# Raw weights cast on GpSimd, and the factors of the mixing fetched on GpSimd's queue

## The chip, the core and the metric

The kernel runs on one core of a Trainium2 chip. The core has five engines with a queue of instructions each: TensorE (PE, matrix products and transposes; its weight loads are shown as PEld), VectorE (DVE), ScalarE (ACT), GpSimd (POOL), and SyncE (SP), which here only issues DMAs. Each queue is worked off in its order; an instruction that waits for a semaphore holds up what stands behind it on the same queue. The metric is the device time of one execution in microseconds, smaller is better.

## The reference

One layer of a hybrid decoder for a prompt of 2048 tokens and 8 sample tokens, model width 1024, float32 in and out:

```python
h = einsum('bsd,de->bse', x, w_in)          # q, k, v and gate of two mixers
# mixer A: 8 heads, banded attention (128) at dilations 1, 4 and 16,
#   the three partial results merged by their softmax denominators
# mixer B: 8 query / 2 key heads, window 128, a learned sink per head
mix = concat([oa * silu(ga), ob * silu(gb)])
y = layer_norm(ALPHA * x + mix @ w_o) * ln_g + ln_b
```

The keys and values are outputs as well. The sample tokens attend to a cache; the 2048 prompt tokens hold nearly all of the work.

## The kernel before, in words

Products of float32 quality are made of three products of a faster format: each operand is split into a high part `h` (a cast to that format) and a low part `l` (the operand less its high part), and `h*h + h*l + l*h` is summed in PSUM. Every weight tile therefore needs a cast and a subtraction before PE can use it.

The kernel has four stages. Up to 244 us it projects the first ten column tiles of the input projection, to about 386 us the values and the sample tokens of mixer A, to about 1062 us runs the attention stage, and then the output projection with the normalisation.

The attention stage is written out by hand (`manual_schedule`): every engine's queue holds its instructions in the order of the program text. Its main loop (lines 1121 to 1151) runs over blocks: for each head pair and each dilation four blocks, 12 blocks for a pair of mixer A (four pairs) and 4 for a pair of mixer B (four pairs). In a block PE makes the scores (L823), DVE masks them and finds the extremes (L831), ACT takes the exponentials (L834), PE transposes them (L853), DVE or ACT copies the transposes from PSUM (L859, L857), and PE multiplies by the values (L874). Each block has four steps; in each step PE is also given a share of other work (`advance`), which is the projection of the remaining tiles (`stream`, products at L629), and then `step()` is called. This first calls `tick`, which calls `raw_step` and issues stores that are due, and then moves each running chain (a Python generator) one `yield` further.

Three of these are touched by the change or by the prediction:

- **Raw weights.** `stream` makes three passes over the tokens, with four, four and three weight tiles; `out_weights` and `late_wo` later need the eight tiles of the output projection. 17 of these tiles come through the class `Parts` in four pieces of 128x256. `raw_step` (L129) keeps up to four pieces (`RAW`) in flight: it has SP load a piece into the buffer `raw` (L142), and three ticks later, when the tile's place is free, DVE casts it into `h` (L137) and POOL subtracts (L138). When PE needs a tile that is not complete yet, the text forces the rest. The first two tiles of a set have places named `gw`, the next ones `gw2` and `gw3`; the tiles of a new set take the places of the old one while its last chunk of tokens is projected.
- **Mixing of a pair of mixer A** (`merge_a`, L1001). From the statistics DVE and ACT compute a factor for each token and dilation; SP stores the factors to DRAM (`fd`, L1028). They are fetched back in eight chunks of 256 tokens, each spread over 64 partitions for each of the two heads: two DMAs of 64 x 3 x 256 numbers a chunk (L1038) into the buffer `F`, of which there are two. POOL multiplies the three partial results by the factors and adds them: five instructions a chunk (L1050, L1052, L1053). After two ticks the fetch of the chunk after next follows, and SP stores the mixed chunk (`ms`, L1058) one tick later.
- **Mixing of a pair of mixer B** (`merge_b`, L944). It has one factor a token, three chunks of 768, 768 and 512 tokens and two DMAs a chunk (L980). POOL multiplies (L990), DVE the second chunk, and all of the last pair.

SP issues all DMAs of the kernel in one queue: besides those named, the tokens of the projection (`gx`, L581), keys, queries and values (L898, L906, L772 to L782), the gates (L175) and the statistics (L935, L940).

Of the kernel before, what the change touches and what calls it, by code (L numbers as in the profile page):

```python
# [18 lines left out]
SEQ = 2048  # L19
# [27 lines left out]
def dram(t, off, ap):  # L47
    return bass.AP(tensor=t.tensor, offset=t.offset + off, ap=[list(a) for a in ap])
# [3 lines left out]
def hymba_step(ctx, tc, xt, xs, xr, wq, wv, wo, tab, msk, ident, diag, sinks, lng, lnb,  # L52
               kca, vca, kcb, vcb, y, kto, vo):
    nc = tc.nc
    V, S, G, T = nc.vector, nc.scalar, nc.gpsimd, nc.tensor
    dma = nc.sync.dma_start
# [36 lines left out]
    def tick(last=False):  # L93
        slot[0] += 1
        raw_step()
        while due and (last or any(d.at <= slot[0] for d in due)):
            now = [d for d in due if last or d.at <= slot[0]]
            due[:] = [d for d in due if d not in now]
            for d in now:
                d.run()  # L100

    def soon(fn, steps=2):
        return Later(fn, steps) if steady else fn()
# [10 lines left out]
    class Parts:  # L114
# [9 lines left out]
        def __iter__(self):  # L124
            while self.left:
                raw_step(True)
            return iter(self.hl)

    def raw_step(now=False):  # L129

        for r in raws:
            r[4] += r[3] is not None
        for _ in range(2):
            if raws and raws[0][0].hl and raws[0][3] is not None and (now or raws[0][4] >= 3):
                p, _, k0, w, _ = raws.popleft()
                h, l = p.hl
                V.tensor_copy(h[:, k0:k0 + 2], w)  # L137
                G.tensor_sub(l[:, k0:k0 + 2], w, h[:, k0:k0 + 2].bitcast(F32))  # L138
                p.left -= 1
        for r in [r for r in islice(raws, RAW) if r[3] is None][:2]:  # L140
            r[3] = at.tile([128, 2, 128], F32, name="raw", bufs=RAW)
            dma(r[3], r[1][:, r[2]:r[2] + 2])  # L142
# [83 lines left out]
    with tc.tile_pool(name="wp", bufs=2) as wp, tc.tile_pool(name="pw", bufs=2) as pw:  # L226
# [13 lines left out]
        def x_of(ci, kt):  # L240
            return [t[:, kt % 2] for t in X5[kt // 2]] if ci == 6 else [t[:, kt] for t in X[ci]]
# [80 lines left out]
        for oi, i in enumerate(order):  # L322
            for ci in range(7):
                if oi == 0 and ci < 6:
                    load_x(ci + 1)
                n = 7 * oi + ci
# [5 lines left out]
                c0, n = CHUNKS[ci]  # L332
# [157 lines left out]
    with xscope, tc.tile_pool(name="spa", bufs=1, reuse_waits="tile") as sp, \  # L490
# [9 lines left out]
        for gi, (h0, w) in enumerate(VG):  # L500
            wvh, wvl = wvp[gi]
            for tb in VO[gi]:
# [19 lines left out]
                for kt in () if new else range(8):  # L522
                    ci = max(i for i in range(7) if CHUNKS[i][0] <= tb * 128)
                    t0 = tb * 128 - CHUNKS[ci][0]
                    a, b = [t[:, t0:t0 + 128] for t in x_of(ci, kt)]
# [418 lines left out]
    def merge_b(job):  # L944

        m, den = job.of.st[:, 0, :, 0], job.of.st[:, 0, :, 1]
        sk = snk[:, 2 * job.of.pair:2 * job.of.pair + 2, None].to_broadcast([128, 2, 16])
        mn = at.tile([128, 2, 16], F32, name="mn", bufs=1)
        w = at.tile([128, 2, 2, 16], F32, name="wts", bufs=1)
        dn = at.tile([128, 2, 16], F32, name="dn", bufs=1)  # L950
        V.scalar_tensor_tensor(mn, sk, -1.0, m, op0=OP.mult, op1=OP.min)
        V.tensor_sub(w[:, 0], mn, m)
        V.tensor_add(w[:, 1], mn, sk)
        S.activation(w, w, AF.Exp)
        yield
        V.tensor_mul(dn, w[:, 0], den)
        V.tensor_add(dn, dn, w[:, 1])
        V.reciprocal(dn, dn)
        V.scalar_tensor_tensor(w[:, 0], w[:, 0], 0.5, dn, op0=OP.mult, op1=OP.mult)
        while where[0] < 3:  # L960
            yield
        pst = ps.tile([128, 512], F32, name="pst", tag="pt", bufs=1)
        T.transpose(pst[:32, :128], w[:, 0].rearrange("p a b -> p (a b)"), idt)
        stT = at.tile([64, 128], F32, name="stT")
        V.tensor_copy(stT[:32], pst[:32, :128])
        yield
        for h in range(2):
            dma(job.of.fd[h, 0].rearrange("(r b i) -> b r i", r=16, b=16),
                stT[16 * h:16 * h + 16].rearrange("n (r i) -> n r i", r=16))
        yield  # L970
        yield
        fd = job.of.fd
        kt, o = 4 + job.of.pair, job.of.o[1]
        Fs = []

        def fetch(c):
            F = at.tile([128, 768], F32, name="F", bufs=2)
            n = min(768, SEQ - 768 * c)
            for a in range(2):
                dma(F[a * 64:a * 64 + 64, :n], dram(fd, a * SEQ + c * 768, [[0, 64], [1, n]]))  # L980
            Fs.append(F[:, :n])

        fetch(0)
        fetch(1)
        yield
        yield
        yield
        for c in range(3):
            cc = slice(c * 768, min(c * 768 + 768, SEQ))
            (V if c == 1 or kt == 7 else G).tensor_mul(o[:, cc], o[:, cc], Fs[c])  # L990
            yield
            if c == 0:
                fetch(2)
            if c == 1:
                yield
            if kt < 6:
                soon(lambda kt=kt, cc=cc, o=o: dma(ms[kt, :, cc], o[:, cc]), 1)
        merged.append(kt)
        resident.append(o)

    def merge_a(job):  # L1001

        fd, oT = job.of.fd, job.of.o
        sc = at.tile([128, 2, 3, 2, 16], F32, name="sc", bufs=1)
        yield
        yield
        dma(sc.rearrange("p a b c e -> p (a b c) e"), job.of.sd.rearrange("a b c (p e) -> p (a b c) e", e=16))
        yield
        yield
        yield  # L1010
        mn = at.tile([128, 2, 16], F32, name="mn", bufs=1)
        dn = at.tile([128, 2, 16], F32, name="dn", bufs=1)
        w = at.tile([128, 2, 3, 16], F32, name="wts", bufs=1)
        V.tensor_tensor(mn, sc[:, :, 0, 0], sc[:, :, 1, 0], op=OP.min)
        V.tensor_tensor(mn, mn, sc[:, :, 2, 0], op=OP.min)
        for pi in range(3):
            V.tensor_sub(w[:, :, pi], mn, sc[:, :, pi, 0])
        S.activation(w, w, AF.Exp)
        yield
        V.tensor_mul(dn, w[:, :, 0], sc[:, :, 0, 1])  # L1020
        for pi in range(1, 3):
            V.tensor_mul(mn, w[:, :, pi], sc[:, :, pi, 1])
            V.tensor_add(dn, dn, mn)
        V.reciprocal(dn, dn)
        for pi in range(3):
            V.scalar_tensor_tensor(w[:, :, pi], w[:, :, pi], 0.5, dn, op0=OP.mult, op1=OP.mult)
        yield
        dma(fd.rearrange("a c (p e) -> p (a c) e", e=16), w.rearrange("p a c e -> p (a c) e"))  # L1028
        yield
        yield  # L1030
        yield
        kt = job.of.pair
        Fs = []

        def fetch(c):
            F = at.tile([128, 3, 256], F32, name="F", bufs=2)
            for a in range(2):
                dma(F[a * 64:a * 64 + 64],  # L1038
                    dram(fd, a * 3 * SEQ + c * 256, [[0, 64], [SEQ, 3], [1, 256]]))
            Fs.append(F)  # L1040

        fetch(0)
        fetch(1)
        yield
        yield
        for c in range(8):
            cc = slice(c * 256, c * 256 + 256)
            F = Fs[c]
            m = oT[PA[0]][:, cc]
            G.tensor_mul(m, m, F[:, 0])  # L1050
            for pi, d in enumerate(PA[1:]):
                G.tensor_mul(F[:, 1 + pi], oT[d][:, cc], F[:, 1 + pi])  # L1052
                G.tensor_add(m, m, F[:, 1 + pi])  # L1053
            yield
            yield
            if c < 6:
                fetch(c + 2)
            soon(lambda kt=kt, cc=cc, m=m: dma(ms[kt, :, cc], m), 1)  # L1058
        ready.append(kt)
# [103 lines left out]
    with tc.tile_pool(name="ol", bufs=1, reuse_waits="tile") as ol:  # L1163
# [7 lines left out]
        for i, tb in enumerate([16] + list(range(16))):  # L1171
# [3 lines left out]
            if tb in first:  # L1175
                x, n = first[tb]
# [159 lines left out]
```

## Time and profile before

| | |
|---|---|
| median of the runs | 1244.24 us (3 runs, 1241.34 to 1249.01) |
| profiled execution | 1243.91 us, span of its instructions 1242.1 us |
| mean granted clock of TensorE | 0.978 |
| POOL's busy time, attention stage (386 to 1062 us) | 176.97 of 676 us |
| PE's busy time, attention stage | 606.41 of 676 us |
| DMA | one queue, 228.66 MB, 184 GB/s from and to HBM over the span |

The page gives busy times of the engines, the span in 40 slices, the chain of work that ended last, and groups of instructions by line. A row of the timeline has the start, the duration, the engine, the line, the operation, output and inputs by the program's names, the count of merged instructions, and in brackets how long the engine stood idle before and what released it. A row of waits has who waited for whom, the total, the number of times and the longest. `SPq` is the queue of SP, which issues DMAs: its duration is that of issuing, not of the transfer. In the windows, each engine's busy time stands with its count of instructions; the numbers after POOL are the granted clock, the share of time that the DMA engines were busy, and GB/s.

### The profile page before, as it was taken

How to read it: one execution, taken by the hardware profiler on the slowest of the kernel's cores; microseconds unless marked ns; L12 is line 12 of the kernel's file. 1: busy time of each engine (PE TensorE's matmuls, PEld its weight loads, DVE VectorE, ACT ScalarE, POOL GpSimd, SP SyncE). 2: the span in 40 equal slices, each digit the busy share in tenths (PEclk: the TensorE clock that was granted, in tenths of full speed). 3: DMA queues.
4: the chain of work that ended last, by engine and by line, in shares of the span. 5: the costliest groups of instructions: out<-in, count | busy, mean ns of one | idle time of the engine just before them, and what ended most of it. 6: DMA issues, size and time to landing. Idle time of an engine off the chain costs nothing.

```text
span 1242.1 us, 23436 instructions
## 1 busy us (share of the span) xinstructions
PE 1149.4 (93%) x8614; PEld 1006.3 (81%) x8614; DVE 566.0 (46%) x1855; ACT 430.9 (35%) x1417; POOL 328.6 (26%) x402
## 2 busy tenths in 40 slices
PE   8999999999998999995999899779899896999997
PEld 7899999979977888984887788668777774688885
DVE  6432001010023565553666546465666774685434
ACT  3200111101103565552555445435554451133221
POOL 2243112120012000045105302540243323175432
PEclk9999999999999999997999999989999997999998
DMA  8745887283686573677466746854896847655621
GB/s 276 240 134 177 256 277 254 81 272 128 213 259 192 180 188 124 156 187 170 143 153 176 217 144 172 199 147 142 204 226 197 273 145 219 180 168 185 199 94 68
DMA packets 206067, 230.15 MB, mean 185 GB/s; under 512 B 34640, under 2 KB 174576, under 8 KB 205568
## 3 DMA queue, kind: packets, MB, share of 16 engines
q1 hardware_dynamic: 205952, 228.66, 63.2%
q8 instruction: 67, 1.10, 0.4%
q14 instruction: 48, 0.39, 0.1%
HBM read 158.52 MB, written 70.07 MB: 184 GB/s over the span
## 4 chain that ended last, share of the span: by engine, by line
PE 65%; DMA 13%; DVE 7%; ACT 5%; issue 4%; POOL 3%; SPq 2%; POOLq 0%; DVEq 0%; ACTq 0%
PE po L672 13%; PE pg L629 11%; PE ps_s L823 7%; PE pv L527 7%; PE ps_pt L853 5%; PE pmm L152 5%; PE ps L152 5%; PE ppt L152 4%; ACT pe L834 4%; PE ps_o L874 4%; DMA F<-fd 4%; PE po L152 3%; DVE pT L859 3%; DVE sm L831 2%; DMA k<-ks 2%
## 5 line engine op out<-in xcount | busy, mean ns | idle before, releaser
L834 ACT ACTIVATE pe<-sm,st 128x256 f32<-128x256 f32 (+1 forms) x512 | 235.6, 461 | 241.4 <-DVE st L831 240.4
L831 DVE CUSTOM_DVE_ANT_0 sm<-ps_s,mk 128x256 f32<-128x256 f32 (+1 forms) x512 | 180.4, 375 | 143.2 <-PE ps_s L823 132.5
L853 PE MATMUL ps_pt<-idt,pe 128*128 128x128 f32 x848 | 140.3, 286 | 48.5 <-DVE pT L859 37.6
L629 PE MATMUL pg<-gx,gw 128*128 128x256 f32 (+1 forms) x1104 | 167.5, 294 | 5.9 <-DMA gx<-xd 2.9
L853 PEld LDWEIGHTS ps_pt<-idt,pe 128*128 128x128 f32 x848 | 90.7, 141 | 73.3 <-DVE pT L859 48.9
L629 PEld LDWEIGHTS pg<-gx,gw 128*128 128x128 f32 x1104 | 142.7, 192 | 7.5 <-DMA gx<-xd 3.5
L859 DVE COPY pT<-ps_pt 128x512 f32<-128x512 f32 x176 | 121.2, 689 | 28.3 <-PE ps_pt L853 26.4
L1050 POOL TENSOR_TENSOR oT<-oT,F 128x256 f32<-128x256 f32 x32 | 23.4, 731 | 347.3 <-ACT pe L834 179.4
L874 PE MATMUL ps_o<-pT,v 128*64 128x128 f32 (+1 forms) x1120 | 106.0, 333 | 0.0
L874 PEld LDWEIGHTS ps_o<-pT,v 128*64 128x64 f32 x1120 | 69.7, 136 | 39.3 <-issue 16.6
L834 ACT ACTIVATION_READ_ACCUMULATOR pe<-sm,st 128x1 f32 x512 | 95.8, 187 | 0.0
L823 PE MATMUL ps_s<-k,qo 64*128 64x256 f32 (+1 forms) x768 | 95.5, 390 | 0.0
L823 PEld LDWEIGHTS ps_s<-k,qo 64*128 64x128 f32 x768 | 69.3, 195 | 13.4 <-issue 1.8
L629 PE MATMUL pg<-gx,gw2h 128*128 128x256 f32 (+1 forms) x368 | 75.1, 292 | 1.2 <-ACT spe L406 1.2
L527 PE MATMUL pv<-wvh,xh 128*128 128x384 f32 (+1 forms) x224 | 69.6, 311 | 0.0
L527 PE MATMUL pv<-wvh,xl 128*128 128x384 f32 (+1 forms) x224 | 69.5, 310 | 0.0
L527 PE MATMUL pv<-wvl,xh 128*128 128x384 f32 (+1 forms) x224 | 69.4, 310 | 0.0
L672 PE MATMUL po<-wl,mho 128*128 128x512 f32 x192 | 59.7, 392 | 0.0
L629 PEld LDWEIGHTS pg<-gx,gw2h 128*128 128x128 f32 x368 | 58.3, 191 | 1.5 <-ACT spe L406 1.5
L629 PE MATMUL pg<-gx,gw2l 128*128 128x256 f32 (+1 forms) x184 | 53.9, 293 | 0.0
L539 ACT ACTIVATE vf<-pv 128x384 f32<-128x384 f32 (+1 forms) x32 | 14.0, 438 | 112.7 <-PE pv L527 62.2
L172 DVE SCALAR_TENSOR_TENSOR th<-th,pg 128x256 f32<-128x256 f32 (+1 forms) x64 | 26.9, 420 | 48.7 <-ACT th L168 48.3
(262 smaller groups left out, 2461.8 us busy)
## 6 DMA issues: line engine op xcount, KB each, us to landing
gx<-xd SPq DMA_DIRECT2D x80, 512.0 KB
F<-fd SPq DMA_DIRECT2D x80, 192.0 KB
gs<-th SPq DMA_DIRECT2D x64, 128.0 KB
v<-vs SPq DMA_DIRECT2D x28, 256.0 KB
xd<-xh SPq DMA_DIRECT2D x12, 512.0 KB
xd<-xl SPq DMA_DIRECT2D x12, 512.0 KB
kc<-in_kca SPq DMA_DIRECT2D x8, 768.0 KB
vc<-in_vca SPq DMA_DIRECT2D x6, 1024.0 KB
```

Of the source, the lines that this page charges most:

```text
L152: T.matmul(p[:, :n], a[:, kt, :], b, start=k == 0, stop=k == 23)
L172: V.scalar_tensor_tensor(th[:, :n], th[:, :n], 1.0, p, op0=OP.add, op1=OP.mult)
L527: T.matmul(p[:, :w], l, r[:, kt, :w], start=k == 0, stop=k == 23)
L629: T.matmul(p[:, :n], a[:, kt, :], b[:, kt % 2, :n], start=kt + e == 0, stop=kt == 7 and e == 2)
L672: T.matmul(p, a, b[:, nh * 4:nh * 4 + 4].rearrange("p a b -> p (a b)"), start=first and k == 0, stop=last and k == end)
L823: T.matmul(s[:, h, n % 4, :w], self.Q[g][r, n % 4 * 128:n % 4 * 128 + 128], self.keys(n)[r], start=True, stop=True)
L831: V.tensor_tensor_reduce(sm[:, :w], self.s[:, h, n % 4, :w], mk[:, MI[self.d], 256 - w:], -0.125, 3.0e38, op0=OP.add, op1=OP.min, accum_out=m)
L834: S.activation(p[:, :w], sm[:, :w], AF.Exp, scale=-1.0, bias=m, accum_out=den)
L853: T.transpose(pt[:, h, j], self.P[h, n][:, a:a + 128], idt)
L859: V.tensor_copy(t, pt)
L874: T.matmul(o[64 * h:64 * h + 64, a:a + 128 * len(ns)], v[:, cv, kv:kv + 64], t[:, h, j:j + len(ns)].rearrange("p a b -> p (a b)"), start=n ...
L1050: G.tensor_mul(m, m, F[:, 0])
```

## The change

Two edits. In `raw_step` the cast of a raw weight piece into its high part is given to POOL (`G`) instead of DVE (`V`), so that POOL does both instructions of a piece, one behind the other. In both `fetch` functions, of `merge_b` and `merge_a`, the DMA that fetches the factors is issued by POOL instead of SP (`dma` is SP's `dma_start`). Loads of the raw pieces, stores of the factors and of the mixed chunks stay on SP; buffers, their number and the order of the text stay as they are.

```diff
@@ -134,7 +134,7 @@
             if raws and raws[0][0].hl and raws[0][3] is not None and (now or raws[0][4] >= 3):
                 p, _, k0, w, _ = raws.popleft()
                 h, l = p.hl
-                V.tensor_copy(h[:, k0:k0 + 2], w)
+                G.tensor_copy(h[:, k0:k0 + 2], w)
                 G.tensor_sub(l[:, k0:k0 + 2], w, h[:, k0:k0 + 2].bitcast(F32))
                 p.left -= 1
@@ -977,7 +977,7 @@
             F = at.tile([128, 768], F32, name="F", bufs=2)
             n = min(768, SEQ - 768 * c)
             for a in range(2):
-                dma(F[a * 64:a * 64 + 64, :n], dram(fd, a * SEQ + c * 768, [[0, 64], [1, n]]))
+                G.dma_start(F[a * 64:a * 64 + 64, :n], dram(fd, a * SEQ + c * 768, [[0, 64], [1, n]]))
             Fs.append(F[:, :n])
@@ -1035,7 +1035,7 @@
         def fetch(c):
             F = at.tile([128, 3, 256], F32, name="F", bufs=2)
             for a in range(2):
-                dma(F[a * 64:a * 64 + 64],
+                G.dma_start(F[a * 64:a * 64 + 64],
                     dram(fd, a * 3 * SEQ + c * 256, [[0, 64], [SEQ, 3], [1, 256]]))
             Fs.append(F)
```

## The prediction

> **What bounds the kernel now.** I read the page's busy table first, then the busy time by stage, then the waits, then the order of time around the longest holes of TensorE (PE).
>
> ```profile
> span 1242.1 us, 23436 instructions
> ...
> PE 1149.4 (93%) x8614; PEld 1006.3 (81%) x8614; DVE 566.0 (46%) x1855; ACT 430.9 (35%) x1417; POOL 328.6 (26%) x402
> ```
>
> PE is the bound: 93% of the span. Nothing that the change touches runs on PE, so it can only fill or widen PE's holes. The attention stage, 386 to 1062 us, is where both edited places run. Three of its windows:
>
> ```profile
> 386.00:520.00 134.00, 129.18 (x1183) 114.43 (x1183) 75.96 (x334) 75.52 (x301) 6.10 (x9) 1.00 0.60 172
> ...
> 520.00:625.00 105.00, 89.75 (x769) 76.88 (x766) 56.75 (x219) 50.85 (x190) 40.46 (x56) 0.93 0.61 158
> ...
> 765.00:850.00 85.00, 68.63 (x552) 57.40 (x553) 45.20 (x164) 37.10 (x135) 36.10 (x55) 0.94 0.70 176
> ...
> sum 676.00, PE 606.41 PEld 517.60 DVE 394.59 ACT 332.97 POOL 176.97; mean PE 67.38 PEld 57.51 DVE 43.84 ACT 37.00 POOL 19.66
> ```
>
> After the times come PE, weight loads, DVE, ACT, POOL, then the granted clock. Before 520 us, with POOL nearly idle, PE loses 5 of 134 us; between 520 and 625 it loses 15 of 105, between 765 and 850 it loses 16 of 85, and the clock is lower there too. These are the stages in which POOL mixes a head pair and a new set of weights is made. The waits inside the attention stage say who held whom:
>
> ```profile
> POOL oT L1050 <- DMA F<-fd: 167.4, 25, 44.7
> ...
> PE ps_pt L853 <- DVE pT L859: 37.6, 38, 7.2
> ...
> DVE gw L137 <- DMA raw<-in_wq: 26.3, 5, 13.2
> ```
>
> and the same holes in order of time, PE, then DVE, then SP:
>
> ```profile
> 577.58 1.12 PE L853 MATMUL ps_pt<-idt,pe 128*128 128x128 f32 x4 [10.25 <-DVE stT L930]
> ...
> 586.53 0.44 PE L853 MATMUL ps_pt<-idt,pe 128*128 128x128 f32 x2 [2.78 <-DVE pT L859]
> ...
> 597.19 0.63 PE L629 MATMUL pg<-gx,gw 128*128 128x256 f32 x4
> ...
> 809.24 1.12 PE L853 MATMUL ps_pt<-idt,pe 128*128 128x128 f32 x4 [7.19 <-DVE pT L859]
> ...
> 814.54 0.44 PE L853 MATMUL ps_pt<-idt,pe 128*128 128x128 f32 x2 [2.43 <-DVE pT L859]
> ...
> 834.69 1.23 PE L629 MATMUL pg<-gx,gw 128*128 128x264 f32 x8
> ```
> ```profile
> 575.37 1.96 DVE L137 CAST gw<-raw 128x256 fp32r<-128x256 f32 x4 [13.18 <-DMA raw<-in_wq]
> ```
> ```profile
> 565.40 3.38 SPq L1038 DMA_DIRECT2D F<-fd  x2
> 568.83 0.59 SPq L1058 DMA_DIRECT2D ms<-oT  x1
> 569.46 1.89 SPq L142 DMA_DIRECT2D raw<-in_wq  x4
> ```
>
> This is one chain. DVE came to its cast (L137) at 562.2 and stood 13.18 us for the raw weights; its copies of transposed probabilities (L859), which PE waits for, stood behind. The raw load left SP only at 569.46, because SP issues in order and stood at factor fetches (L1038) that need a buffer from POOL, which in turn waited 167.4 us in all for factors. PE reads the new weights only at 597.19 and 834.69: the holes come from DVE's place in the order, not from a need of PE.
>
> **The change, part by part.** First the cast: each raw load has one, 36 + 32 = 68 in all, and they leave DVE and go on POOL, each just before its subtraction. SP's rows of the loads, and POOL's rows nearest to such a cast:
>
> ```profile
> L142 SPq DMA_DIRECT2D raw<-in_wq x36: 328/382/1544, 382.4 to 826.4; - x36
> L142 SPq DMA_DIRECT2D raw<-in_wo x32: 327/376/1495, 903.8 to 1036.2; - x32
> ```
>
> ```profile
> L1052 POOL TENSOR_TENSOR F<-oT,F 128x256 f32<-128x256 f32 x64 | 47.3, 739 | 0.0
> ...
> L174 POOL COPY sgS<-th 128x8 f32<-128x8 f32 x8 | 1.5, 190 | 30.7 <-DVE th L172 30.7
> ...
> L365 POOL MEMSET z<- 128x1088 f32 x1 | 1.0, 1007 | 20.7 <-PE ppt L152 20.7
> ...
> L365 POOL MEMSET z<- 128x256 f32 x1 | 0.3, 312 | 0.0
> ```
>
> The two memsets give (1007-312)/832 = 0.84 ns an element; from the copy of 8, 190 + 248 x 0.84 = 0.40 us a cast, an estimate between 0.31 (memset) and 0.74 (two inputs). A subtraction has the shape of L1052, 0.74 us; cast and subtraction are 1.14 us, four of them, the first weight tile of a set, 4.5 us. The other side is that DVE no longer waits for raw loads at all. POOL waits in its place, with later subtractions and mixing behind it, which PE needs later.
>
> Second, the fetches: 64 (L1038) and 24 (L980) leave SP and are issued by POOL.
>
> ```profile
> L1038 SPq DMA_DIRECT2D F<-fd x64: 579/606/1767, 518.3 to 940.3; - x64
> ```
> ```profile
> L980 SPq DMA_DIRECT2D F<-fd x24: 450/587/1302, 958.0 to 1052.8; - x24
> ```
> ```profile
> 518.35 2.58 SPq L1038 DMA_DIRECT2D F<-fd  x4
> ...
> 756.37 2.57 SPq L1038 DMA_DIRECT2D F<-fd  x4
> ```
> ```profile
> 525.57 0.73 POOL L1050 TENSOR_TENSOR oT<-oT,F 128x256 f32<-128x256 f32 x1 [118.03 <-ACT pe L834]
> ...
> 529.25 0.73 POOL L1050 TENSOR_TENSOR oT<-oT,F 128x256 f32<-128x256 f32 x1
> ...
> 574.78 0.72 POOL L1050 TENSOR_TENSOR oT<-oT,F 128x256 f32<-128x256 f32 x1 [2.79 <-DMA F<-fd]
> ```
>
> No row shows a DMA issued by POOL; call its time on POOL d. SP's 0.6 is the low bound. For the high one, 1.2 stretched as if POOL stood while DVE is busy (394.59 of 676 us, 58%): 1.2/0.42 = 2.9. I take 1.2, twice SP's row and near it, since a POOL instruction as small as the copy of 8 costs only 0.19. The Trainium skill, "DMA: Bandwidth & Descriptors", section "Specifications", puts the first byte at about 1 us for GpSimd's DMA and 0.6 for SP's; with d = 1.0 from it, an estimate, the sum below would have about 1 us less of costs. No row here shows it.
>
> A factor took 525.57 - 518.35 - 2 x 0.6 = 6.0 us from issue to use, and a chunk of the mix takes 529.25 - 525.57 = 3.68 us. At present the last of the eight chunks begins 49.2 us after the first, 7.0 us a chunk. After the change POOL issues two DMAs for each chunk: the pace is the larger of 2d + 3.68 = 6.1 and, with two buffers, (2d + 6.0 + 3.68)/2 = 6.0. The eight chunks and the first weight tile are then done at 518.35 + 6.0 + 8 x 3.68 + 4.5 + 16d = 558.3 + 16d, and for the second hole, from 756.37, at 796.3 + 16d. With 1.2 that is 577.5 and 815.5.
>
> When does PE need them? The clock is the last piece:
>
> ```profile
> 578.00:592.00 14.00, 11.01 (x69) 9.36 (x69) 6.67 (x25) 5.58 (x20) 6.51 (x9) 0.79 0.61 164
> ...
> 810.00:820.00 10.00, 7.57 (x42) 5.87 (x42) 2.78 (x6) 0.93 (x4) 6.63 (x12) 0.70 0.38 108
> ```
>
> After a hole PE worked at 0.79 and 0.70: 11.01 x 0.21 and 7.57 x 0.30, 2.3 us each. The holes were 10.25 + 2.78 = 13.0 and 7.19 + 2.43 = 9.6. Without them PE needs the tiles at 597.2 - 15.3 = 581.9 and 834.7 - 11.9 = 822.8. Both are met at d = 1.2; the gain begins to shrink at d = 1.48 and 1.66, and is gone at 2.43 and 2.40. So **-15.3 and -11.9 us**. The cover of the new POOL work is that margin, 4.4 and 7.3 us.
>
> The smaller terms have these rows: PE at the first weights, DVE's copies of queries, and the end of the stage on DVE and SP.
>
> ```profile
> 397.32 0.48 PE L629 MATMUL pg<-x,gw3h 128*128 128x264 f32 x2 [1.68 <-DVE gw3h L137]
> ```
> ```profile
> L800 DVE COPY qo<-q 128x512 f32<-128x512 f32 x48 | 24.3, 507 | 0.0
> ```
> ```profile
> 1041.21 0.69 DVE L137 CAST wo7h<-raw 128x256 fp32r<-128x256 f32 x2 [2.45 <-DMA raw<-in_wo]
> ```
> ```profile
> 1052.35 1.09 SPq L980 DMA_DIRECT2D F<-fd  x2
> ```
>
> At 397 PE already waits for a cast; four casts in line with subtractions add 4 x 0.40 = **+1.6** (none, if DVE's queue was what delayed them). DVE's copies of queries may meet POOL's issues: four mixes of 8 x 6.1 us are 195 of 676 us, 14 of the 48 copies, 2.4/6.1 of them beside a DMA for half of d: **+3.3**, bounds 0 and 14 x 1.2 = 17. In the last merge DVE's 2.45 us at 1041 goes, and the fetch at 1052 takes 2 x 1.2 instead of 1.09: **-1.2**, from -2.5 to +2. SP loses 88 x 0.6 = 53 us of issues, which PE never waited for directly; the stores of mixed heads (L1058), which wait for POOL, stay on SP.
>
> Sum: -15.3 - 11.9 + 1.6 + 3.3 - 1.2 = -23.5. The profiled span becomes 1218.6, its execution (1243.91 with 1.8 around the span) 1220.4; it lay 0.3 below the median of the runs shown, so the forecast is **1221**, with a range of its own of 1212 to 1228.
>
> **The rivals.** (1) The wait only moves, from DVE to PE's products, because the factors land no sooner. For it: POOL already spends 167.4 us waiting for them, and the stores on SP still couple raw loads to POOL. If landing takes 9 us instead of 6, the pace is (2.4 + 9 + 3.68)/2 = 7.5, the tiles are ready at 518.35 + 2.4 + 9 + 3.68 + 7 x 7.5 + 4.5 = 590.4 and at 828.4: 8.5 and 5.6 us of the gains stay lost, the sum is -9.4, the time 1235. A d of 1.8 comes to the same by the sums above (tiles at 587.1 and 825.1, 16 copies of queries beside an issue), one of 2.0 to 1247. Against it: on SP a fetch stood behind other loads, on POOL it would not. The Trainium skill, "DMA: Bandwidth & Descriptors", section "Rules for kernel authors", says that spreading issues over queues brings no bandwidth, since all share 16 engines, and saves only issue time; by it this rival is the outcome.
>
> (2) Slower: issuing becomes POOL's bound, from about d = 2.2. At d = 2.9 a chunk takes 9.5 us, the tiles are ready at 604.7 and 842.7, 7.5 and 8.0 later than PE reads them today. The second and fourth mix take 8 x (9.5 - 7.0) = 20 us longer each, SP stands at their stores, and loads behind them have no slack:
>
> ```profile
> 711.26 2.07 PE L629 MATMUL pg<-gx,gw 128*128 128x256 f32 x8 [2.40 <-DMA gx<-xd]
> ```
>
> Half of it on PE gives +20; the mixes cover 22 copies of queries, 0.61 of them beside an issue for 1.45 us, +19; the first weights and the end +4. Together +58, the time 1302; the same sum at d = 2.5 gives 1277. For it: casts that take 0.29 us alone show that POOL and DVE hold each other up:
>
> ```profile
> L137 DVE CAST gw<-raw x16: 280/296/829, 575.4 to 824.8; 128x256 fp32r<-128x256 f32 x16
> ```
>
> Against it: POOL's own 64 factor products keep to 739 ns beside a busy DVE. The Trainium skill, "SBUF — State Buffer", section "SBUF: two separate sides", describes it as a trap: DVE copies keep GpSimd from writing its descriptors, 620 ns becoming 3100. No run here shows it.
>
> (3) Better: the small gaps behind L859 (37.6 us less the 12.4 counted above) shrink too, 1200 to 1212.
>
> **How the numbers follow.** Forecast 0.46, rival 1 0.31, rival 2 0.18, rival 3 0.05. One per cent, 12 us, is about what a measurement tells from no change: the bounds are 1232 and 1257. The forecast and rival 3 are faster, with 0.09 of rival 1: 0.60. The rest of rival 1 lies within: 0.22. Slower is rival 2: 0.18. The range 1206 to 1262 leaves out half of rival 3 and 0.15 of rival 2, under 2 in 10.
>
> **What would show it.** Right: no wait of DVE at L137, PE's holes at 567 to 577 and 802 to 809 gone, the clock near 1.00 there, raw loads of the second set leaving SP when the sixth chunk is mixed, at 518.35 + 6.0 + 6 x 3.68 + 14 x 1.2 = 563 instead of 569.46, DMA instructions of POOL near 1.2 us. Wrong: PE's L629 waiting for POOL's L137 or L138 (rival 1, or 2 if the issues on POOL take over 2.2 us), a chunk's pace of 7 us or more, or SP standing longer at L1058 than now.

## The result, and the profile after

| | median | runs | profiled execution | span | mean clock |
|---|---|---|---|---|---|
| before | 1243.97 us | 4 (1241.34 to 1249.01) | 1243.91 us | 1242.1 us | 0.978 |
| after | 1212.9 us | 4 (1212.23 to 1215.88) | 1213.31 us | 1211.5 us | 0.988 |

The ratio of after to before is 0.975, with a 95% interval of 0.9715 to 0.9785: the change saves 2.5%, about 31 us. Timed again later beside three other kernels on one chip, it was 1210.79 us against 1242.84 (0.9753, 0.9722 to 0.9784).

The head of the page after, the two lines that were shown of before:

```profile
span 1211.5 us, 23415 instructions
...
PE 1143.3 (94%) x8614; PEld 1001.7 (83%) x8614; DVE 553.9 (46%) x1787; ACT 429.8 (35%) x1417; POOL 409.8 (34%) x558
```

POOL has 156 more instructions, which are the 68 casts and the 88 fetches, and is busy 81 us longer. It is still the engine with the least to do, now just behind ACT. The stages of the attention, in the same windows as before (times, then PE, weight loads, DVE, ACT, POOL, then granted clock, DMA share, GB/s):

```profile
386.00:520.00 134.00, 130.25 (x1190) 115.34 (x1190) 73.60 (x326) 75.42 (x301) 10.66 (x20) 1.00 0.59 174
520.00:625.00 105.00, 102.76 (x929) 89.36 (x925) 61.65 (x254) 59.46 (x227) 55.12 (x86) 1.00 0.78 190
...
765.00:850.00 85.00, 79.36 (x667) 66.99 (x665) 49.65 (x183) 44.97 (x160) 40.04 (x71) 1.00 0.76 194
```

Between 520 and 625 us PE now loses 2.2 us where it lost 15; from 765 to 850 (which, with everything earlier by some 15 us, holds a little more of the following work) it loses 5.6 instead of 16. The clock is 1.00 in both windows instead of 0.93 and 0.94. The waits of the attention stage (who waited for whom, total, times, longest):

```profile
PE ps_pt L853 <- DVE pT L859: 24.3, 35, 1.1
...
POOL gw2h L137 <- DMA raw<-in_wq: 18.0, 3, 13.1
```

No wait of DVE at L137 is left, and PE's longest wait for DVE's copies has come down from 7.2 us to 1.1. The wait did not move to POOL: the 13.1 us that POOL stands at L137 are at 387 us, at the first weights, where it stood 14.8 us for DVE's cast before. At the two holes POOL goes to its first cast without a wait, because by then it has worked through its mixing and the weights have landed; it waits for later pieces alone, 0.5 us behind the first and 2.9 and 2.2 behind the second. POOL's longest wait and its first casts at the two holes, then PE at the first hole, in order of time:

```profile
387.11 0.40 POOL L137 CAST gw2h<-raw 128x256 fp32r<-128x256 f32 x1 [13.05 <-DMA raw<-in_wq]
...
576.62 0.40 POOL L137 CAST gw<-raw 128x256 fp32r<-128x256 f32 x1
...
796.79 0.39 POOL L137 CAST gw<-raw 128x256 fp32r<-128x256 f32 x1
```
```profile
577.24 0.66 PE L853 MATMUL ps_pt<-idt,pe 128*128 128x128 f32 x4
...
581.39 0.63 PE L629 MATMUL pg<-gx,gw 128*128 128x256 f32 x4
582.23 0.66 PE L853 MATMUL ps_pt<-idt,pe 128*128 128x128 f32 x4 [0.21 <-DVE pT L859]
```

PE goes through without a hole and reads the new weights at 581.39, 4.4 us after the first of them was cast. The cast itself comes later than before (576.62 against DVE's 575.37), and yet PE reads the weights 15.8 us sooner: it was never short of weights, but of copies.

Where the 30.6 us of span went can be added up, from the start of the span, the start of PE's scores (L823) in five of the 64 blocks, counted from 1, the issue of the last stores (L692) and the end of the span. Each column is the length of a stretch, and its difference from before in brackets, of one execution of each kernel; the two kernels with half of the change are those of the next section.

| stretch | before | after | cast alone | fetches alone |
|---|---|---|---|---|
| start to block 22 | 563.67 | 564.05 (+0.4) | 563.42 (-0.3) | 562.41 (-1.3) |
| 22 to 24 (first hole) | 36.04 | 19.73 (-16.3) | 19.35 (-16.7) | 34.85 (-1.2) |
| 24 to 45 | 195.88 | 196.14 (+0.3) | 195.53 (-0.4) | 197.63 (+1.8) |
| 45 to 47 (second hole) | 33.46 | 18.88 (-14.6) | 18.49 (-15.0) | 28.91 (-4.6) |
| 47 to 64 | 184.03 | 185.07 (+1.0) | 186.26 (+2.2) | 186.66 (+2.6) |
| 64 to the last stores | 225.22 | 220.36 (-4.9) | 221.49 (-3.7) | 227.88 (+2.7) |
| last stores to the end | 3.80 | 7.27 (+3.5) | 3.86 (+0.1) | 7.26 (+3.5) |
| span | 1242.1 | 1211.5 (-30.6) | 1208.4 (-33.7) | 1245.6 (+3.5) |

The two holes give 30.9 of the 30.6 us. The rest, -4.9 and +3.5 at the end and +1.7 in between, nearly cancels.

### The profile page after: what moved, and what is told of

It reads as the page before. It is cut to its first block, busy times and chain, and to the rows that moved or that the text cites. A ratio compares the mean times of both kernels' runs of the same rounds, so it can differ in the third digit from the quotient of the medians.

```text
span 1211.5 us, 23415 instructions
## 1 busy us (share of the span) xinstructions
PE 1143.3 (94%) x8614; PEld 1001.7 (83%) x8614; DVE 553.9 (46%) x1787; ACT 429.8 (35%) x1417; POOL 409.8 (34%) x558
## 4 chain that ended last, share of the span: by engine, by line
PE 72%; DMA 9%; DVE 6%; ACT 6%; issue 3%; SPq 1%; POOL 1%; DVEq 0%; POOLq 0%; ACTq 0%
PE po L672 13%; PE pg L629 13%; PE ps_s L823 8%; PE pv L527 7%; PE ps_pt L853 7%; PE ps_o L874 5%; PE pmm L152 5%; PE ps L152 5%; PE ppt L152 5%; ACT pe L834 5%; DMA gx<-xd 3%; PE po L152 3%; DVE pT L859 2%; DVE sm L831 1%; DMA wvf<-in_wv 1%
## 5 line engine op out<-in xcount | busy, mean ns | idle before, releaser
L629 PE MATMUL pg<-gx,gw 128*128 128x256 f32 (+1 forms) x1104 | 165.7, 292 | 6.9 <-DMA gx<-xd 3.8
L853 PE MATMUL ps_pt<-idt,pe 128*128 128x128 f32 x848 | 139.5, 285 | 25.0 <-DVE pT L859 24.3
L629 PEld LDWEIGHTS pg<-gx,gw 128*128 128x128 f32 x1104 | 140.9, 190 | 8.6 <-DMA gx<-xd 4.9
L1038 POOL DMA_DIRECT2D F<-fd x64 | 41.2, 646 | 227.7 <-DMA fd<-wts 220.8
L823 PE MATMUL ps_s<-k,qo 64*128 64x256 f32 (+1 forms) x768 | 91.9, 379 | 0.0
L823 PEld LDWEIGHTS ps_s<-k,qo 64*128 64x128 f32 x768 | 67.0, 189 | 12.6 <-issue 1.9
L629 PE MATMUL pg<-gx,gw2h 128*128 128x256 f32 (+1 forms) x368 | 74.7, 291 | 1.2 <-ACT spe L406 1.2
L629 PEld LDWEIGHTS pg<-gx,gw2h 128*128 128x128 f32 x368 | 57.8, 189 | 1.5 <-ACT spe L406 1.5
L629 PE MATMUL pg<-gx,gw2l 128*128 128x256 f32 (+1 forms) x184 | 53.7, 292 | 0.0
L260 POOL TENSOR_TENSOR wl<-w,wh 128x512 fp32r<-128x512 f32 x18 | 24.2, 1360 | 84.2 <-DVE wh L259 84.2
```

The lines of the kernel that those rows point to most:

```text
L260: (V if between else G).tensor_sub(l[:, k0:k0 + 4], w, h[:, k0:k0 + 4].bitcast(F32))
L629: T.matmul(p[:, :n], a[:, kt, :], b[:, kt % 2, :n], start=kt + e == 0, stop=kt == 7 and e == 2)
L823: T.matmul(s[:, h, n % 4, :w], self.Q[g][r, n % 4 * 128:n % 4 * 128 + 128], self.keys(n)[r], start=True, stop=True)
L853: T.transpose(pt[:, h, j], self.P[h, n][:, a:a + 128], idt)
L1038: G.dma_start(F[a * 64:a * 64 + 64], dram(fd, a * 3 * SEQ + c * 256, [[0, 64], [SEQ, 3], [1, 256]]))
```

## The experiments

The theory was the prediction's chain: DVE's place at L137 makes the holes, and the fetches on SP make the raw load, and so DVE's cast, late. Two rivals were open after the result: that only one of the two edits does the work, and that the margin POOL has is much smaller than it looks. The first four kernels ran on one chip, where before was 1241.45 us (1237.08 to 1245.32, 13 runs).

### The cast alone

```diff
-                V.tensor_copy(h[:, k0:k0 + 2], w)
+                G.tensor_copy(h[:, k0:k0 + 2], w)
```

> Only the cast moves to POOL; the factors are fetched on SP's queue as before. Theory (the two large holes of PE come from DVE standing at its cast L137): SP's loop of fetches is as late as before, so the last chunk of the first mix ends near 578.5 us and the first weight tile is ready near 583, about 1 us after PE can use it; the second hole goes altogether. Holes of 10.25 and 7.19 us on PE become 0 to 2 us, the time is 1214 to 1219. Rival (the late factors on SP are the cause, and the cast alone only moves the wait to PE's products): PE waits 5 us or more at L629 at both places, the time is 1230 or more.

Measured: 1209.58 us (1208.16 to 1211.69), ratio 0.9745 (0.9718 to 0.9773). Faster than the theory gave. SP's queue, POOL and PE of this kernel at the place of the first hole:

```profile
565.05 3.23 SPq L1038 DMA_DIRECT2D F<-fd  x2
568.33 0.59 SPq L1058 DMA_DIRECT2D ms<-oT  x1
568.97 2.26 SPq L142 DMA_DIRECT2D raw<-in_wq  x4
```
```profile
577.70 0.40 POOL L137 CAST gw<-raw 128x256 fp32r<-128x256 f32 x1
```
```profile
580.77 0.63 PE L629 MATMUL pg<-gx,gw 128*128 128x256 f32 x4
```

SP stands at the fetches as before, and the raw load leaves it at 568.97, as late as the 569.46 of before. Yet PE has no hole there: it reads the weights at 580.77, 2.7 us after the first cast ended. The late raw load did no harm by itself. It did harm because DVE stood in line for it with PE's copies behind.

### The fetches alone

```diff
-                dma(F[a * 64:a * 64 + 64, :n], dram(fd, a * SEQ + c * 768, [[0, 64], [1, n]]))
+                G.dma_start(F[a * 64:a * 64 + 64, :n], dram(fd, a * SEQ + c * 768, [[0, 64], [1, n]]))
...
-                dma(F[a * 64:a * 64 + 64],
+                G.dma_start(F[a * 64:a * 64 + 64],
```

> Only the fetches move to POOL; DVE casts as before. Theory: DVE still comes to its cast near 562 and stands until the raw load lands; SP issues it near 565 instead of 569.5, so the hole of PE near 570 shrinks from 10.3 to about 6 us, the one near 805 from 7.2 to about 4, the time is 1230 to 1237. Rival: the holes are gone, the time is 1220 or less.

Measured: 1243.62 us (1239.73 to 1247.82), ratio 1.002 (1.000 to 1.004). Both missed: there is no gain. DVE and PE of this kernel:

```profile
570.12 0.58 DVE L137 CAST gw<-raw 128x256 fp32r<-128x256 f32 x2 [9.20 <-DMA raw<-in_wq]
```
```profile
573.72 1.12 PE L853 MATMUL ps_pt<-idt,pe 128*128 128x128 f32 x4 [7.65 <-DVE stT L930]
...
584.17 0.69 PE L853 MATMUL ps_pt<-idt,pe 128*128 128x128 f32 x2 [4.05 <-DVE pT L859]
...
807.20 1.11 PE L853 MATMUL ps_pt<-idt,pe 128*128 128x128 f32 x4 [5.86 <-DVE pT L859]
...
819.37 0.66 PE L853 MATMUL ps_pt<-idt,pe 128*128 128x128 f32 x4 [1.39 <-DVE pT L859]
...
1043.49 0.37 PE L963 MATMUL pst<-idt,wts 128*32 128x128 f32 x1 [5.06 <-DVE wts L959]
```

```profile
563.17 0.33 SPq L1058 DMA_DIRECT2D ms<-oT  x1
563.54 2.46 SPq L142 DMA_DIRECT2D raw<-in_wq  x4
```

The raw load does leave 5.9 us earlier, at 563.54 (1.3 of them because this execution is ahead by as much at block 22), and DVE stands 9.20 us instead of 13.18. But the holes shrink only from 13.0 to 11.7 us and from 9.6 to 7.3, because DVE reaches the cast at 560.9 and the raw load still waits on SP for a store of mixed heads (L1058), which waits for POOL. SP's waits at that line, in before and in after, show that its standing has moved from the fetches to the stores:

```profile
SPq L1058 <- POOL oT L1053: 9.3, 5, 3.3
```
```profile
SPq L1058 <- POOL oT L1053: 59.3, 21, 12.9
```

With the fetches alone it is 67.4 us. By the table 5.8 us are won in the two holes, 5.8 are lost over the rest of the way to the last stores, where after wins 3.2, and 3.5 behind them. What loses the 5.8 wasn't followed; this execution was also 3.7 us above the kernel's median.

### POOL's time per fetch stretched

Ahead of each of the 64 fetch DMAs of mixer A POOL also clears the half buffer that the DMA then fills, once or twice. The DMA then writes over the zeros; what grows is POOL's time for a fetch, from 0.62 us to 1.7 or 2.5. The 24 fetches of mixer B are as in after.

```diff
             for a in range(2):
+                G.memset(F[a * 64:a * 64 + 64], 0.0)
                 G.dma_start(F[a * 64:a * 64 + 64],
```

> The changed kernel with a memset of the half buffer F by POOL ahead of each fetch DMA: POOL's time for an issue goes from 0.62 to about 1.7 us, the data are the same. By the prediction's formula a chunk's pace goes from the 6.8 us seen to about 7.3, the first weight tiles are ready some 6 us later, which is beyond the margins (0 and 3 us): PE waits 6 and 3 us more at L629, the time is about 1221. Rival (POOL's time for issues is covered, factors landing are the pace): 1212 to 1216.

Measured: 1220.61 us (1214.15 to 1221.47), ratio 0.9823 (0.9791 to 0.9855). The time is as expected, the way is not. No wait of PE for POOL at L629 stands in the trace. This execution is 3.1 us ahead of after's at block 22, and POOL begins its casts at 577.23, 0.6 us later than in after: against PE they come 3.7 us later. PE reads the weights at 578.30, 0.7 us after the first piece was cast, where after had 4.4 us to spare. Most of the clearing, some 16 us a mix, fits into the time in which POOL would have waited for the factors anyway; the rest is covered, just, because PE needs one piece and not the whole tile. The loss is elsewhere on PE, whose waits for tokens grow from 3.8 us in after to 9.2:

```profile
692.88 1.65 PE L629 MATMUL pg<-gx,gw 128*128 128x256 f32 x6 [4.87 <-DMA gx<-xd]
...
830.05 1.00 PE L629 MATMUL pg<-gx,gw 128*128 128x256 f32 x6 [2.27 <-DMA gx<-xd]
```

These are loads of tokens, issued by SP behind the stores of mixed heads that wait for POOL's mixing.

With two such lines, the second identical to the first:

> The same with two memsets: POOL's time for an issue about 2.4 us, where the prediction saw the whole gain at the two holes gone. Pace 8.5 us a chunk, tiles 16 us later, PE waits about 16 and 13 us at L629 and some 14 us in the two other mixes: about 1256. Rival (the margin is larger than worked out, as PE needs a tile in pieces): 1225 to 1240.

Measured: 1258.31 us (1247.91 to 1263.74), ratio 1.0128 (1.0073 to 1.0182): slower than before. POOL's first cast, then PE of this kernel:

```profile
586.98 0.40 POOL L137 CAST gw<-raw 128x256 fp32r<-128x256 f32 x1
```
```profile
587.43 1.60 PE L629 MATMUL pg<-gx,gw 128*128 128x256 f32 x4 [6.82 <-POOL gw L137]
...
707.87 1.22 PE L629 MATMUL pg<-gx,gw 128*128 128x256 f32 x4 [10.05 <-DMA gx<-xd]
...
832.33 2.50 PE L629 MATMUL pg<-gx,gw 128*128 128x264 f32 x8 [6.57 <-POOL gw L137]
```

Now the wait for POOL is there, 6.82 and 6.57 us where 16 and 13 were expected, and the waits for tokens are 20.2 us in all. PE began 0.05 us after the first of the four casts ended (586.98 + 0.40): it needs one piece of the tile, not the whole tile as the prediction had counted. The second rival's mechanism is real, at a price per issue that the unstretched kernel doesn't come near.

### Both beside each other, and what is left

Four more kernels ran on one chip; before was 1242.84 us there (1237.83 to 1248.47, 11 runs). The first two are after and the cast alone once more, since the span of the cast alone was 3.1 us shorter.

> The changed kernel beside the kernel with the cast alone, on one chip, so that the two are compared directly. If the move of the fetches costs time at the end of the kernel (theory: 3.5 us more between the last store issued at L692 and the end), this one is about 3 us above the cast alone (1212.9 against 1209.6 where they were timed apart) and its span ends 7.3 us after that store, against 3.8. If the difference came only from two timings apart, the two agree within 1 us.

> The cast alone on GpSimd, fetches on SP. Theory: 1209 to 1211 us, 3.8 us from the last store to the end of the span. Rival (the two kernels are alike): the same time as the changed kernel within 1 us.

Measured: 1210.79 us (1207.03 to 1215.19; ratio 0.9753, 0.9722 to 0.9784) for after, 1211.1 us (1205.96 to 1215.94; 0.9753, 0.9720 to 0.9786) for the cast alone. The two can't be told apart: one kernel's runs spread over 8 to 10 us here, and a difference of 3 us disappears in that. In the second executions the stretches of the two holes came out as in the table: 19.73 and 18.91 us in after, 19.34 and 18.55 in the cast alone. The stretch from block 64 to the last stores agrees to 1.0 us (220.2 and 222.5). The other three moved by up to 4.2 us, so that a difference of 1 to 3 us there says nothing. What the traces also show, in each of the four, is the stretch behind the last stores. Start of their issue in after, after again, the cast alone and the cast alone again:

```profile
1204.23 0.99 SPq L692 DMA_DIRECT2D out_y<-xo  x2
```
```profile
1199.92 0.99 SPq L692 DMA_DIRECT2D out_y<-xo  x2
```
```profile
1204.54 0.99 SPq L692 DMA_DIRECT2D out_y<-xo  x2
```
```profile
1206.67 0.99 SPq L692 DMA_DIRECT2D out_y<-xo  x2
```

The spans end at 1211.5, 1207.2, 1208.4 and 1210.5: 7.3 us later twice where POOL issues the fetches, 3.8 us twice where SP does. Whether that goes with any DMA that POOL issues was the next question. In the cast alone, one small load of the beginning was given to POOL:

```diff
-        dma(snk, dram(sinks, 0, [[0, 128], [1, 8]]))
+        G.dma_start(snk, dram(sinks, 0, [[0, 128], [1, 8]]))
```

> The cast alone, with one small load of the kernel's beginning (128x8, L321) issued by GpSimd instead of SP: the only DMA that GpSimd issues. Theory (that GpSimd issued any DMA lengthens the kernel's end): about 3.5 us above the cast alone, 1212 to 1214 us, with 7.3 us between the last store at L692 and the end of the span. Rival (the length goes with the 88 fetches, or with how late the last of them is): as the cast alone within 1 us, 3.8 us at the end.

Measured: 1212.78 us (1207.58 to 1214.33), ratio 0.9756 (0.9726 to 0.9786); by the time alone this says nothing, by the trace the theory falls:

```profile
1201.93 0.99 SPq L692 DMA_DIRECT2D out_y<-xo  x2
```

with a span of 1205.8, 3.9 us later. One early DMA of POOL doesn't lengthen the end; the 88 fetches do. The traces show what takes the time: at the end of the program (L1313) each engine drains its queue, and SP waits there for POOL. POOL's drains at that line (ns, shortest, median and longest; then first and last start) in after, in the cast alone and in this kernel:

```profile
L1313 POOLq DRAIN  x3: 40/102/7874, 1202.8 to 1211.2; - x3
```
```profile
L1313 POOLq DRAIN  x3: 39/78/657, 1203.1 to 1208.1; - x3
```
```profile
L1313 POOLq DRAIN  x3: 40/93/757, 1200.5 to 1205.5; - x3
```

The longest drain is 7.87 us in all five traces with the 88 fetches on POOL, 0.66 to 0.67 in the four where POOL issues no DMA, and 0.76 with the one early DMA. In after SP has come to the end at 1207.4 and goes on at 1210.9, when POOL's drain is over. The added 7.2 us are 0.08 us for each of the 88, and the one added 0.10: by this estimate it is their number that counts, and not their bytes (the one has 4 KB, each of the 88 some 190) or how late the last of them comes. No kernel with a number in between was run.

The last kernel asks after the 22.0 us, in 32 waits, that PE still stands behind DVE's copies in the cast alone. There, the copies of queries were given to ACT:

```diff
-            V.tensor_copy(a, b)
+            S.activation(a, b, AF.Copy)
```

> The cast alone, with DVE's 48 query copies (L800, 0.42 to 0.52 us, 24.9 us in all) made by ScalarE instead. Theory (what is left of TensorE's waits for DVE's copies L859, 22.0 us over 32 waits, comes from query copies queued ahead of them): the waits fall to under 10 us and the time to 1197 to 1203 us. Rival (the waits come from DVE's minima L831, or ScalarE's 48 added copies of about 0.6 us delay its exponentials L834 as much): 1207 to 1215 us, with waits of TensorE for ScalarE in place of those for DVE.

Measured: 1209.88 us (1206.42 to 1213.19), ratio 0.9734 (0.9704 to 0.9764). The rival holds as to the time. The wait in the cast alone, and with the copies on ACT:

```profile
PE ps_pt L853 <- DVE pT L859: 22.0, 32, 1.1
```
```profile
PE ps_pt L853 <- DVE pT L859: 25.7, 31, 1.2
```

The waits stay though DVE has 48 copies less, so most of them don't come from copies of queries ahead of them. The part of the rival that had waits for ACT in their place isn't seen. None of these kernels beats the changed one by more than the runs' spread.

## Why the prediction was right, and where it was off

The forecast was 1221 us, faster; measured were 1212.9 and 1210.8. The direction, the place and the mechanism on DVE and PE held. The gain forecast was 8 us too small, and one link of the chain was wrong.

**The holes.** Forecast -15.3 and -11.9 us, measured -16.3 and -14.6 (the table above). Filling a hole also gave back the clock behind it, as the two added 2.3 us had it: the windows show 1.00. Of the 2.7 us more that the second gave, 1.8 are two further waits of PE for DVE's copies in the same stretch of before (0.61 us at 823.40 and 1.23 at 826.27), which the prediction's lines left out; after has one of 0.20 there. The rest is open.

**The chain: "The raw load left SP only at 569.46, because SP issues in order and stood at factor fetches (L1038)".** True of the trace, but not what the holes hang on. With the fetches left on SP the raw load is as late and the holes are gone; with only the fetches moved, it leaves 5.9 us earlier and 11.7 of 13.0 us stay. The step that carried everything was the first: DVE's place in the order. The prediction put both edits into one sum and gave neither a price of its own, so it didn't see that one of them was worth nothing. Of its signs of right, the load was to leave at 563 and left at 565.28; and one of its signs of wrong is there, SP standing longer at L1058 (59.3 us instead of 9.3), at no price on PE's holes. That the cast on DVE could also have been placed later in its own queue wasn't tried; the runs show that it has to leave its place, not that it has to leave DVE.

**d, POOL's time for an issue.** Taken as 1.2 us, with bounds of 0.6 and 2.9. The groups of after:

```profile
L1038 POOL DMA_DIRECT2D F<-fd x64: 612/618/867, 518.3 to 903.8; - x64
```
```profile
L137 POOL CAST gw<-raw x16: 391/398/402, 576.6 to 808.1; 128x256 fp32r<-128x256 f32 x16
```

A fetch costs POOL 0.618 us, SP's price (0.606) and so the low bound; with a wait of 0.30 ahead of each pair it is 1.54 us a chunk. The value chosen was twice too high: nothing in the trace of before spoke for anything above SP's row but a guess of stretching. The cast is 0.40 us, as worked out from the memsets.

**The landing and the pace.** Landing was taken as 6.0 us, from the end of a pair's issues to the first use. Counted from the start of each DMA's own issue, the median is 7.3:

```profile
DMA to landing us min/median/max: 5.1/7.3/11.8
```

Counted as the prediction did, from the end of a pair's issues to the landing of its last, it is 7.3 too, over 32 pairs from 5.5 to 11.2. The first and the last of the first mix's eight chunks on POOL begin here:

```profile
525.63 0.73 POOL L1050 TENSOR_TENSOR oT<-oT,F 128x256 f32<-128x256 f32 x1 [4.59 <-ACT pe L834]
...
572.95 0.74 POOL L1050 TENSOR_TENSOR oT<-oT,F 128x256 f32<-128x256 f32 x1 [2.73 <-DMA F<-fd]
```

Before the last one POOL waits 2.73 us for factors, and 53.1 us in 23 waits over the four mixes: the pace is set by landing and not by the issues. The chunks began 47.3 us apart in all, 6.8 us a chunk instead of the 6.1 forecast and the 7.0 of before. Rival 1's arithmetic, that factors land no sooner, was nearly right, and the casts of the first tile were ready at 581.3 instead of 577.5. Two errors cancelled: POOL's issues were cheaper and the landing longer than counted. By the prediction's own count its margin was then 0.1 us and not 4.4, so that the first hole closed in full was luck as to that count. Rival 1 failed at the other end of the comparison, an assumption that it shared with the forecast: the tile was counted as needed whole; PE needs its first piece, which was there at 577.0 for a read at 581.4. The Trainium skill, "DMA: Bandwidth & Descriptors", section "Rules for kernel authors", on which that rival leaned, says that issuing from several queues saves issue time alone. The kernel with the fetches alone agrees: 88 issues of 0.6 us moved to another queue, and no time gained (1.002). That the rival would follow from it didn't hold, since the gain comes from the cast.

**The costs.** +1.6 us for the first weights and +3.3 for copies of queries were forecast, 4.9 in all; all stretches outside the holes and up to block 64 show +1.7, which is within what they move by themselves. The wait of 1.68 us for `gw3h` at 397 is gone rather than longer, the case that the prediction had put in brackets. The copies of queries rose from 24.3 us in all to 24.9. This pair of rows shows DVE's copy, then POOL's issues at the same time:

```profile
640.42 0.42 DVE L800 COPY qo<-q 128x512 f32<-128x512 f32 x1
```
```profile
640.30 1.29 POOL L1038 DMA_DIRECT2D F<-fd  x2 [0.30 <-POOL oT L1053]
```

Neither is longer than alone (0.42 and 1.28). Of five copies that ran beside an issue of POOL and nothing else of it, four took 0.42 us and one 0.56. Beside POOL's products the copy is often longer:

```profile
560.99 0.98 DVE L800 COPY qo<-q 128x512 f32<-128x512 f32 x1
```
```profile
560.96 0.73 POOL L1050 TENSOR_TENSOR oT<-oT,F 128x256 f32<-128x256 f32 x1 [2.13 <-DMA F<-fd]
```

The mechanism of rival 2, with the Trainium skill's trap in "SBUF — State Buffer", section "SBUF: two separate sides", isn't seen in this case: the longest of the 64 issues took 0.867 us, where the page has 3.1 for a DMA. Nor does the mix as a whole show lateness: with SP issuing the fetches, POOL comes to its casts at 577.70, no sooner than the 576.62 of after. As the stretched kernels show, the arithmetic of rival 2 was sound in kind: at about 2.5 us for each fetch of mixer A the kernel is slower than before, 1258 us, where the rival had 1277 for d = 2.5.

**The end of the stage.** Forecast -1.2 us, measured -4.9 up to the last stores. In before, PE waits 4.65 us for DVE's `wts` (L959), which stood behind the cast of `wo7h`:

```profile
1043.98 0.37 PE L963 MATMUL pst<-idt,wts 128*32 128x128 f32 x1 [4.65 <-DVE wts L959]
```

With the fetches alone it still waits 5.06 there, with the cast alone 0.78, and in after not at all. The prediction saw DVE's 2.45 us at that cast, and not what was queued behind it. Behind the last stores 3.5 us were added that no step had: POOL's drain.

**The sum.** Against the -23.5 us forecast, the terms differ by -1.0 and -2.7 (holes), -3.7 (end of the stage), -3.2 (costs that didn't arise) and +3.5 (behind the last stores): -7.1, which makes -30.6. The -3.2 is within the spread of those stretches; the holes, the last stretch and the drain came again in after's second execution.

## What to carry to other kernels

An instruction that waits for a DMA belongs on an engine that comes to it after the load has landed, or whose next work nobody needs soon: it isn't the lateness of the load that costs, but what stands in line behind the instruction that waits for it. When a change has two edits, price each alone from the profile; here one carried all of the gain and the other none. And before counting a margin, look at which piece of a tile the reader takes first.

## What the runs showed of the hardware

Three things weren't expected. A DMA of 64 x 3 x 256 numbers costs POOL 0.62 us to issue, much as it costs SP (0.606), and 0.61 to 0.79 beside DVE's copies of queries. A copy of 128x512 numbers on DVE, 0.42 us alone, took up to 0.98 beside POOL's tensor instructions but 0.42 to 0.56 beside its issues alone. And DMAs that POOL issues are paid for again at the end: with the 88 fetches POOL's last drain takes 7.87 us instead of 0.66, and the span ends 7.3 us after the issue of the last stores instead of 3.8 to 3.9, in after, after again, the fetches alone (1238.34 to 1245.6) and both stretched kernels; with a single DMA from POOL the drain takes 0.76 us and the end is as before.
